# Row halves of TensorE taken in turn in a time mix, and value rows split three tiles ahead in an expert layer

## Chip, cores and metric

One core of one Trainium2 chip runs the whole program. The metric is the device time of one execution in microseconds; lower is better. Three timed executions of the kernel before took 3079.56, 3082.31 and 3094.72 us.

## The reference

Two transformer blocks over 512 tokens of width 1024, in float32. The first has attention, a convolution branch and a product-key expert layer (16,384 experts, 8 heads, top 16). The second has a linear-recurrence time mix (RWKV-7), a sparse attention (NSA), a gated merge and a convolutional feed-forward. Two parts matter here:

```python
# expert layer, for a chunk of 128 tokens
u = peer_u[e]                                  # e: 16 experts for each of 8 heads
h = gelu(einsum('cd,chkd->chk', xc, u))
return einsum('chk,chkd->cd', g * h, peer_v[e])

# time mix, for every token
sa = einsum('bhvk,bhk->bhv', state, a_t)
state = state * w_t + sa[..., None] * b_t + v_t[..., None] * k_t
y_t = einsum('bhvk,bhk->bhv', state, r_t)
```

The expert layer is computed densely for three of the four token tiles (all 16,384 experts, with a gate matrix that is zero nearly everywhere) and by gathers for the fourth. The time mix is computed in chunks of 128 tokens: products of the keys, queries and decays under a triangular mask, the inverse of a triangular matrix for each chunk and head, and a state that goes from chunk to chunk.

## The kernel before, in words

The program is written with a tile framework. Each engine has its own queue in order; the order of the queues is planned at compile time by a simulated time line over the program order, and tiles with a number of buffers (`bufs`) make their next user wait until an old one is free. PSUM is cut into eight banks: four with the tag `pb`, two `mm`, two `po`.

Matmuls at full precision split their operands in a high and a low part (float32r) and take three products, `mm3` (L264 to L266). A plain float32 matmul appears in the trace as two records, each with its own weight load.

**Expert layer** (`peer`). The 16,384 experts are 128 tiles of 128. In the loop at the end of `peer`, a group of four tiles at a time, `up` makes the weighted gelu of the next group (by matmuls L264 to L266, or from a tile that was computed ahead and stored, `gh_d`), splits it (L817, L818) and calls `slot_up`, a gather and a dot product for the fourth token tile (L779, L788). Then `v_split(et + 1)` splits the next tile of value rows: ScalarE casts two halves (L676), GpSimd and VectorE subtract (L677), and the next load is issued on SyncE's queue (L666). The split tiles have two buffers each (`vh`, `vl`, L673); the raw rows have three. Then 18 matmuls (L844) accumulate the tile into six banks, and `slot_down` gathers a value row for each token and adds it (L796). `weights(gi + 1)` loads the gates of the next group (L800), with two buffers. Before the loop, the first split is done when the routing of the last token tile is known (L743).

**Time mix** (`Rwkv`). Heads of 64 come in pairs, so a tile of 128 rows holds two heads, the even one (`par` 0) in rows 0 to 63 and the odd one in rows 64 to 127.
- `pair` makes the inputs of two heads for all four chunks. At its end (L1464 to L1471) each `par` takes a bank, four matmuls over 64 rows, and a masked multiply into `LT`.
- `invert` inverts the triangular blocks: by VectorE up to 32 x 32, then by matmuls over 32 rows (L1529, L1534, L1536) and over 64 rows (L1545, L1549). The 32-row part goes over two quads (rows 0 to 63, and 64 to 127) and, in each, over two chunks with a bank each.
- `front` prepares a chunk without the state; its helper `lower` (L1580) does three masked products, each for both `par` in turn: a bank, four matmuls over 64 rows (L1586), a masked multiply on VectorE (L1588), and a `yield`. `times_v` (L1597) uses the results. `back` does what needs the state. `chunks` runs `back` of one chunk in turns with `front` of the next.

Beside it, projections for the sparse attention (L264 to L266, `side` and `plain` in `block2`) are given out in portions behind each chunk, and the keys of the attention are prepared (`Nsa.keys`: L1765 to L1822) once `invert` has freed its memory.

Of the kernel before, what the change touches and what calls it, by code (L numbers as in the profile page):

```python
# [9 lines left out]
F32R = mybir.dt.float32r  # L10
# [8 lines left out]
P = 128  # L19
S = 512  # L20
D = 1024
# [515 lines left out]
SD = ND * P  # L537
NE = 128
GE = 4
VRAW = 3  # L540
NA = 68
TB = 32
NSLOT = 128
# [14 lines left out]
def peer(c, st, st_u, last):  # L558
# [20 lines left out]
    for half, cs in enumerate(HALVES):  # L579
# [3 lines left out]
        for k in range(KD):  # L583
            if half and k % 4 == 0:
                tp = c.bank()
            hn, h, lo = c.t2("hn")[:, 0:256], xh[k][:, cs], xl[k][:, cs]
# [42 lines left out]
    for hd in range(8):  # L629
        for half in range(2):  # L630
            if 2 * hd + half < NQH:
                ps = first[2 * hd + half][0]
            else:
                ps = c.bank("mm", 2)
# [25 lines left out]
    ng = NE // GE  # L660
# [7 lines left out]
    def v_split(et):  # L668

        if et >= NE:  # L670
            return
        r = vraw.pop(et)
        h, lo = (vp.tile([P, D], F32R, name=f"v{n}{et}", tag=f"v{n}", bufs=2) for n in "hl")  # L673
        for e in range(2):
            s = slice(e * 512, (e + 1) * 512)
            nc.scalar.copy(h[:, s], r[:, s])  # L676
            (nc.vector if e % 2 else nc.gpsimd).tensor_sub(lo[:, s], r[:, s], h[:, s])  # L677
        vsplit[et] = (h, lo)
        v_load(et + VRAW)


    for i in order:
# [55 lines left out]
        if i == order[-1]:  # L738
            esE.close()
            vp = esB.open("c8", 2)  # L740
            for et in range(VRAW):
                v_load(et)
            v_split(0)  # L743

        gf, gs = c.sm("gf", [P, P], bufs=1), c.sm("gs", [P, 2, P], F16, bufs=2)
        nc.scalar.activation(gf, tr[:, 2 * P:3 * P], AF.Copy, scale=GSCALE)
# [49 lines left out]
        nc.vector.scalar_tensor_tensor(acc, v, ghs[gi][:, s:s + 1], acc, op0=OP.mult, op1=OP.add)  # L796

    def weights(gi):
        wt = c.sm("wt", [P, GE * SD], bufs=2).rearrange("p (b e t) -> p b e t", b=SD // TB, e=GE)
        nc.sync.dma_start(wt, w_d[:, :, gi * GE:(gi + 1) * GE, :].rearrange("b p e t -> p b e t"))  # L800
        return wt

# [17 lines left out]
        slot_up(gi, e)  # L820

    ahead(NA - NB)
    wt = weights(0)
    for e in range(GE):
        up(0, e, wt)
    ahead(NB)
    acc = esB.open("gat", 1, side="right").tile([P, D], F32, name="acc", tag="acc")
    nc.gpsimd.memset(acc, 0.0)

    outs = [[c.bank(("po", "pb", "pb")[i]) for _ in range(2)] for i in range(ND)]  # L830
    for gi in range(ng):
        if gi + 1 < ng:
            wt = weights(gi + 1)
        for e in range(GE):
            et = gi * GE + e
            if gi + 1 < ng:
                up(gi + 1, e, wt)
            v_split(et + 1)
            vs, ps = vsplit.pop(et), acts.pop(et)
            for i in range(ND):  # L840
                ts = slice(i * P, (i + 1) * P)
                for n, (a, v) in enumerate(((0, 0), (0, 1), (1, 0))):
                    for half in range(2):
                        nc.tensor.matmul(outs[i][half], ps[a][:, ts], vs[v][:, half * 512:(half + 1) * 512],  # L844
                                         start=et == 0 and n == 0, stop=et == NE - 1 and n == 2)
            slot_down(gi, e)
# [511 lines left out]
class Rwkv:  # L1358
# [52 lines left out]
    def pair(self, cj, r, k, v):  # L1411
# [49 lines left out]
        nc.gpsimd.tensor_mul(k, k, e2)  # L1461
        nc.gpsimd.tensor_mul(a, a, e2)
        nc.vector.scalar_tensor_tensor(kk, kk, -1.0, e3, op0=OP.mult, op1=OP.mult)
        for par in range(2):  # L1464
            rows = slice(par * 64, par * 64 + 64)
            ps = self.bank()
            for n in range(4):
                cs = slice(n * P, (n + 1) * P)
                nc.tensor.matmul(ps[:, cs], a[rows, cs], kk[rows, cs], start=True, stop=True)
            nc.vector.tensor_mul(self.LT[g][:, :, par * 4 + j], ps.rearrange("p (n t) -> p n t", n=4),  # L1470
                                 up_s[:, None, :].to_broadcast([P, 4, P]))  # L1471
        for w, t in enumerate((kk, r, k, a, v, rkr)):
# [3 lines left out]
    def invert(self, g):  # L1476
# [38 lines left out]
        for n0 in (0, 2):  # L1515
            st = []
            for n in (n0, n0 + 1):
                u0, pt = n * 8, PT[n]
                q64 = self.sm("q64", [P, 8, 64], bufs=2)
                nc.gpsimd.memset(q64, 0.0)  # L1520
                for b in range(4):
                    s = slice(b * 32, b * 32 + 32)
                    nc.gpsimd.tensor_copy(q64[s, :, (b % 2) * 32:(b % 2) * 32 + 32], Qc[s, u0:u0 + 8, :])
                    nc.vector.tensor_copy(pt[s, :, s], Pc[s, u0:u0 + 8, :])
                st.append((u0, pt, q64, c.bank("po", 2), self.sm("zz", [P, 8, 32], bufs=2)))
            for q0, q1 in quads:
                for u0, pt, q64, z1, zz in st:
                    for u in range(8):
                        nc.tensor.matmul(z1[q1, u * 32:(u + 1) * 32], pt[q0, u, q1], Qc[q0, u0 + u, :], start=True, stop=True)  # L1529
                    nc.vector.tensor_copy(zz[q1], z1[q1, 0:256].rearrange("p (u i) -> p u i", u=8))  # L1530
            for q0, q1 in quads:
                for u0, pt, q64, z1, zz in st:
                    for u in range(8):
                        nc.tensor.matmul(z1[q1, 256 + u * 32:256 + (u + 1) * 32], Pc[q1, u0 + u, :], zz[q1, u, :],  # L1534
                                         start=True, stop=True)
                        nc.tensor.matmul(z1[q0, 256 + u * 32:256 + (u + 1) * 32], zz[q1, u, :], Pc[q1, u0 + u, :],  # L1536
                                         start=True, stop=True)
                    nc.vector.tensor_copy(q64[q1, :, 0:32], z1[q1, 256:512].rearrange("p (u i) -> p u i", u=8))
                    nc.vector.tensor_copy(pt[q0, :, q1], z1[q0, 256:512].rearrange("p (u i) -> p u i", u=8))
            z3s = []  # L1540
            for u0, pt, q64, z1, zz in st:
                z3, z6 = c.bank("po", 2), self.sm("z6", [P, 8, 64], bufs=2)
                z3s.append((z3, z6))
                for u in range(8):
                    nc.tensor.matmul(z3[hi, u * 64:(u + 1) * 64], pt[lo, u, hi], q64[lo, u, :], start=True, stop=True)  # L1545
                nc.vector.tensor_copy(z6[hi], z3[hi, :].rearrange("p (u i) -> p u i", u=8))
            for (u0, pt, q64, z1, zz), (z3, z6) in zip(st, z3s):
                for u in range(8):
                    nc.tensor.matmul(z3[lo, u * 64:(u + 1) * 64], z6[hi, u, :], pt[hi, u, hi], start=True, stop=True)  # L1549
                nc.vector.tensor_copy(pt[lo, :, hi], z3[lo, :].rearrange("p (u i) -> p u i", u=8))  # L1550
                nc.sync.dma_start(self.pt_d[u0 // 8][g], pt.rearrange("p u t -> p (u t)"))
        self.pp = pp

    def front(self, g, n):
# [24 lines left out]

        def lower(lhs, rhs, msk, tag):  # L1580
            r = []
            for par in range(2):
                rows = slice(par * 64, par * 64 + 64)
                ps = self.bank()
                for j in range(4):
                    nc.tensor.matmul(ps[:, j * P:(j + 1) * P], lhs[rows, j], rhs[rows, j], start=True, stop=True)  # L1586
                t = self.sm(tag, [P, 4, P], 4 if tag == "rb" else 2)
                nc.vector.tensor_mul(t, ps.rearrange("p (j t) -> p j t", j=4), msk[:, None, :].to_broadcast([P, 4, P]))  # L1588
                r.append(t)
                yield  # L1590
            return r
# [484 lines left out]
```

## Time and profile before

| what | value |
|---|---|
| median of three timed executions | 3082.31 us |
| the profiled execution | 3063.27 us |
| its span, first to last instruction | 3061.3 us |
| TensorE, VectorE, GpSimd, ScalarE busy | 2855.0, 2309.1, 1806.8, 1208.4 us |
| mean granted TensorE clock | 0.957 |

Busy time of an engine is the union of its instructions; the ends of matmuls are modelled, so they lie over each other, and the time from one matmul's start to the next one's is what a matmul takes of TensorE. PE is TensorE's matmul, PEld its weight load, DVE VectorE, ACT ScalarE, POOL GpSimd, SP SyncE; a q behind it is the queue itself. "A <- B" among the waits is A's engine standing idle until B.

The stages are, from the span's start: the first block's attention and convolution and the routing up to about 840 us, the expert loop to about 1660, the time mix's inputs to about 1980, its inversion and chunks to about 2320, the sparse attention to about 2540, then the merge and the feed-forward.

### The profile page before, as it was taken

Reading aid. Unit: us, or ns where it says so; the run is one execution under the profiler, and the core shown is the slowest. Engines: PE = TensorE matmul, PEld = TensorE weight load, DVE = VectorE, ACT = ScalarE, POOL = GpSimd, SP = SyncE. Lnnn points to the kernel's source line nnn. Section 1 sums busy time; section 2 is a strip of 40 time slices with the busy share of each in tenths; the row PEclk is TensorE's granted clock in tenths of the full one; section 3 lists DMA queues with packets and bytes.
Section 4 is the critical chain, followed back from the end, with each engine's and each line's share of the span. In section 5 each row is a group of like instructions: output and inputs, shape, how many; then the busy total and the mean of one; then the engine's idle time right before and its main releaser. Section 6 shows DMA issues by size and latency. Waiting matters only on the chain. (4 is left out here: it accounts for less than half of the span.)

```text
span 3061.3 us, 42565 instructions
## 1 busy us (share of the span) xinstructions
PE 2855.0 (93%) x15507; PEld 2433.8 (80%) x15507; DVE 2309.1 (75%) x3734; ACT 1208.4 (39%) x2077; POOL 1806.8 (59%) x1231
## 2 busy tenths in 40 slices
PE   6789997889999999999999899899999998999998
PEld 5557897779978888888887677688887877888887
DVE  7985899997188999999998688968345874477721
ACT  4444334456333333333334432211225764444431
POOL 5544465543667888888885376623347754554444
PEclk9789998999999999999999999998999999999999
DMA  3101244446799999999996555453753226322232
GB/s 131 41 14 57 77 129 127 173 156 249 237 338 316 327 335 335 323 324 341 332 336 212 177 161 165 139 172 104 222 159 99 76 70 214 120 90 93 93 96 76
DMA packets 270918, 554.01 MB, mean 181 GB/s; under 512 B 41394, under 2 KB 147890, under 8 KB 268916
## 3 DMA queue, kind: packets, MB, share of 16 engines
q1 hardware_dynamic: 219264, 370.91, 37.8%
q0 software_dynamic: 36864, 134.23, 12.0%
q10 hardware_dynamic: 14580, 46.15, 4.2%
q8 instruction: 122, 2.00, 0.3%
q14 instruction: 88, 0.72, 0.1%
HBM read 464.77 MB, written 83.89 MB: 179 GB/s over the span
## 5 line engine op out<-in xcount | busy, mean ns | idle before, releaser
L247 POOL TENSOR_TENSOR wl<-wr,wh 128x1024 fp32r<-128x1024 f32 x319 | 812.9, 2550 | 557.8 <-ACT wh L245 297.9
L245 ACT CAST wh<-wr 128x1024 fp32r<-128x1024 f32 x319 | 334.7, 1050 | 611.5 <-PE mm L265 201.3
L788 DVE CUSTOM_DVE_ANT_0 ur<-ur,hnt 128x1024 f32<-128x1024 f32 x128 | 216.8, 1695 | 74.2 <-DMA ur<-in_u,eix 72.9
L779 POOL DMA_INDIRECT ur<-in_u,eix x128 | 169.5, 1324 | 63.7 <-DVE hc L788 34.4
L677 POOL TENSOR_TENSOR vl<-vr,vh 128x512 fp32r<-128x512 f32 x128 | 190.9, 1492 | 23.6 <-ACT vh L676 18.1
L677 DVE TENSOR_TENSOR vl<-vr,vh 128x512 fp32r<-128x512 f32 x128 | 183.4, 1433 | 25.8 <-issue 16.8
L796 DVE SCALAR_TENSOR_TENSOR acc<-vr,hc,acc 128x1024 f32<-128x1024 f32 x128 | 193.5, 1512 | 1.8 <-DMA vr<-in_vrow,eix 1.7
L779 POOL DMA_INDIRECT vr<-in_vrow,eix x128 | 155.5, 1215 | 47.1 <-issue 24.0
L676 ACT CAST vh<-vr 128x512 fp32r<-128x512 f32 x256 | 145.6, 619 | 76.2 <-issue 31.1
L844 PE MATMUL pb<-vl,ah 128*128 128x512 f32 x512 | 168.9, 397 | 0.0
L844 PE MATMUL pb<-vh,al 128*128 128x512 f32 x512 | 166.4, 395 | 0.0
L844 PE MATMUL pb<-vh,ah 128*128 128x512 f32 x512 | 163.1, 399 | 2.4 <-ACT ah L817 2.4
L766 PE MATMUL pb<-og,o 128*128 128x128 f16 x768 | 105.8, 296 | 41.6 <-DVE og L761 41.2
L766 PEld LDWEIGHTS <-o 128*128 128x128 f16 x768 | 82.7, 119 | 59.6 <-DVE og L761 28.5
L768 ACT ACTIVATE wb<-pb 128x512 f32<-128x512 f32 x96 | 98.9, 1139 | 71.6 <-PE pb L766 71.1
L353 DVE SCALAR_TENSOR_TENSOR acc<-hp,vecs,acc 128x512 f32<-128x512 f32 x100 | 115.8, 1173 | 0.7
L844 PEld LDWEIGHTS pb<-vh,ah 128*128 128x128 f32 x512 | 97.3, 190 | 23.7 <-ACT ah L817 2.7
L844 PEld LDWEIGHTS pb<-vl,ah 128*128 128x128 f32 x512 | 97.2, 190 | 23.0
L844 PEld LDWEIGHTS pb<-vh,al 128*128 128x128 f32 x512 | 97.2, 190 | 22.9
L758 DVE TENSOR_TENSOR o<-iota,sl 128x1024 f16<-128x1024 f16 x96 | 105.4, 1126 | 11.1 <-ACT sl L737 6.9
L1927 POOL TENSOR_TENSOR prob<-prob,nz 128x128 f32<-128x128 f32 (+3 forms) x128 | 88.6, 724 | 39.4 <-DVE nz L1924 27.6
L1152 DVE TENSOR_TENSOR tot<-tot,sq 128x512 f32<-128x512 f32 x11 | 17.0, 1548 | 112.9 <-ACT sq L1149 112.9
(1404 smaller groups left out, 8991.0 us busy)
## 6 DMA issues: line engine op xcount, KB each, us to landing
wr<-in_ws SPq DMA_DIRECT2D x191, 512.0 KB
wr<-in_uT SPq DMA_DIRECT2D x128, 512.0 KB
vr<-in_vrow SPq DMA_DIRECT2D x128, 512.0 KB
w_d<-wb ACTq DMA_DIRECT2D x12, 2048.0 KB
wt<-w_d SPq DMA_DIRECT2D x32, 768.0 KB
gh_d<-gh ACTq DMA_DIRECT2D x68, 192.0 KB
gh<-gh_d SPq DMA_DIRECT2D x68, 192.0 KB
rd_d<-z SPq DMA_DIRECT2D x24, 256.0 KB
```

Of the source, the lines that this page charges most:

```text
L245: c.nc.scalar.copy(h, r)
L247: eng.tensor_sub(lo, r, h)
L353: nc.vector.scalar_tensor_tensor(acc[j], hp[:, tap:tap + S], w[:, tap:tap + 1], acc[j], op0=OP.mult, op1=OP.add)
L676: nc.scalar.copy(h[:, s], r[:, s])
L677: (nc.vector if e % 2 else nc.gpsimd).tensor_sub(lo[:, s], r[:, s], h[:, s])
L758: nc.vector.tensor_tensor(o, iota4[:, None, :, :].to_broadcast(shape), by4(sl[:, a, ts]), op=OP.is_equal)
L766: nc.tensor.matmul(wp[:, u * P:(u + 1) * P], o2[:, q, :, u], og[n][:, q, :, u], start=n == 0, stop=n == 1)
L768: nc.scalar.activation(wb[:, :, t4:t4 + 4].rearrange("p e t -> p t e"), wp.rearrange("p (t e) -> p t e", t=4), AF.Copy, scale=1.0 / GSCALE)
L779: nc.gpsimd.indirect_dma_start(out=t, out_offset=None, in_=src, in_offset=bass.IndirectOffsetOnAxis(ap=eix[:, s:s + 1], axis=0))
L788: nc.vector.tensor_tensor_reduce(out=u, in0=u, in1=hnt, scale=1.0, scalar=0.0, op0=OP.mult, op1=OP.add, accum_out=hc[:, s:s + 1])
L796: nc.vector.scalar_tensor_tensor(acc, v, ghs[gi][:, s:s + 1], acc, op0=OP.mult, op1=OP.add)
L844: nc.tensor.matmul(outs[i][half], ps[a][:, ts], vs[v][:, half * 512:(half + 1) * 512], start=et == 0 and n == 0, stop=et == NE - 1 and n == 2)
```

## The change

Four places in the time mix put the two row halves in turn: in `pair` and in `lower` both halves take their bank first, the matmuls alternate between the halves, and the two masked multiplies come behind all of them; in `invert` the 32-row matmuls go over two "turns", each with a different quad for each of the two chunks, alternating from matmul to matmul, with the copies behind. In the expert layer the value rows are split three tiles ahead instead of one, with four buffers instead of two, three splits before the loop instead of one, and the gates are loaded two groups ahead instead of one.

```diff
+VAHEAD = 3
...
-        h, lo = (vp.tile([P, D], F32R, name=f"v{n}{et}", tag=f"v{n}", bufs=2) for n in "hl")
+        h, lo = (vp.tile([P, D], F32R, name=f"v{n}{et}", tag=f"v{n}", bufs=VAHEAD + 1) for n in "hl")
...
-            v_split(0)
+            for et in range(VAHEAD):
+                v_split(et)
...
-        wt = c.sm("wt", [P, GE * SD], bufs=2).rearrange("p (b e t) -> p b e t", b=SD // TB, e=GE)
+        wt = c.sm("wt", [P, GE * SD], bufs=3).rearrange("p (b e t) -> p b e t", b=SD // TB, e=GE)
...
-    wt = weights(0)
+    wts = [weights(0), weights(1)]
...
-        if gi + 1 < ng:
-            wt = weights(gi + 1)
+        if gi + 2 < ng:
+            wts.append(weights(gi + 2))
...
-            v_split(et + 1)
+            v_split(et + VAHEAD)
...
-        for par in range(2):
-            rows = slice(par * 64, par * 64 + 64)
-            ps = self.bank()
-            for n in range(4):
-                cs = slice(n * P, (n + 1) * P)
+        pss = [self.bank() for _ in range(2)]
+        for n in range(4):
+            cs = slice(n * P, (n + 1) * P)
+            for par, ps in enumerate(pss):
+                rows = slice(par * 64, par * 64 + 64)
                 nc.tensor.matmul(ps[:, cs], a[rows, cs], kk[rows, cs], start=True, stop=True)
+        for par, ps in enumerate(pss):
             nc.vector.tensor_mul(self.LT[g][:, :, par * 4 + j], ps.rearrange("p (n t) -> p n t", n=4),
...
-            for q0, q1 in quads:
-                for u0, pt, q64, z1, zz in st:
-                    for u in range(8):
+            turns = [[(quads[(a + b) % 2], st[a]) for a in range(2)] for b in range(2)]
+            for turn in turns:
+                for u in range(8):
+                    for (q0, q1), (u0, pt, q64, z1, zz) in turn:
                         nc.tensor.matmul(z1[q1, u * 32:(u + 1) * 32], pt[q0, u, q1], Qc[q0, u0 + u, :], start=True, stop=True)
+                for (q0, q1), (u0, pt, q64, z1, zz) in turn:
                     nc.vector.tensor_copy(zz[q1], z1[q1, 0:256].rearrange("p (u i) -> p u i", u=8))
-            for q0, q1 in quads:
-                for u0, pt, q64, z1, zz in st:
-                    for u in range(8):
+            for turn in turns:
+                for u in range(8):
+                    for (q0, q1), (u0, pt, q64, z1, zz) in turn:
                         nc.tensor.matmul(z1[q1, 256 + u * 32:256 + (u + 1) * 32], Pc[q1, u0 + u, :], zz[q1, u, :],
                                          start=True, stop=True)
+                    for (q0, q1), (u0, pt, q64, z1, zz) in turn:
                         nc.tensor.matmul(z1[q0, 256 + u * 32:256 + (u + 1) * 32], zz[q1, u, :], Pc[q1, u0 + u, :],
                                          start=True, stop=True)
+                for (q0, q1), (u0, pt, q64, z1, zz) in turn:
                     nc.vector.tensor_copy(q64[q1, :, 0:32], z1[q1, 256:512].rearrange("p (u i) -> p u i", u=8))
...
-            for par in range(2):
-                rows = slice(par * 64, par * 64 + 64)
-                ps = self.bank()
-                for j in range(4):
+            pss = [self.bank() for _ in range(2)]
+            for j in range(4):
+                for par, ps in enumerate(pss):
+                    rows = slice(par * 64, par * 64 + 64)
                     nc.tensor.matmul(ps[:, j * P:(j + 1) * P], lhs[rows, j], rhs[rows, j], start=True, stop=True)
+            for ps in pss:
                 t = self.sm(tag, [P, 4, P], 4 if tag == "rb" else 2)
                 nc.vector.tensor_mul(t, ps.rearrange("p (j t) -> p j t", j=4), msk[:, None, :].to_broadcast([P, 4, P]))
```

## Rows read from the trace of the kernel before

**Rows 1.** Stage and length, us; busy PE, PEld, DVE, ACT, POOL; clock, DMA share, GB/s.
```profile
840.00:1660.00 820.00, 802.61 (x3783) 693.75 (x3784) 757.34 (x789) 288.74 (x534) 664.84 (x438) 0.99 0.91 323
...
1780.00:1880.00 100.00, 100.00 (x508) 83.35 (x507) 88.84 (x92) 28.98 (x47) 77.20 (x53) 1.00 0.57 164
1880.00:1980.00 100.00, 84.27 (x406) 68.17 (x405) 92.17 (x116) 21.94 (x38) 57.24 (x37) 0.90 0.53 151
1980.00:2080.00 100.00, 96.90 (x918) 81.80 (x917) 71.31 (x123) 17.04 (x27) 33.44 (x28) 0.92 0.46 152
...
2180.00:2320.00 140.00, 137.68 (x855) 119.01 (x855) 50.11 (x114) 41.23 (x74) 65.40 (x46) 0.96 0.59 172
```
**Rows 2.** TensorE's groups, 1780 to 2300: xcount | busy us, mean ns | idle before.
```profile
L1586 PE MATMUL pb<-ar,ck 64*128 64x128 f32 x384 | 49.3, 293 | 0.0
...
L1469 PE MATMUL pb<-kk,a 64*128 64x128 f32 x128 | 14.3, 293 | 3.2 <-DVE kk L1463 3.2
...
L1536 PE MATMUL po<-c4y,zz 32*32 32x32 f32 x256 | 10.5, 193 | 0.0
...
L1529 PE MATMUL po<-c4y,LT 32*32 32x32 f32 x256 | 10.1, 194 | 0.0
```
**Rows 3.** TensorE's time line in pieces: start, duration, line, shape, records merged.
```profile
2023.32 0.48 PE L1586 MATMUL pb<-ar,ck 64*128 64x128 f32 x2
2023.73 0.59 PE L1529 MATMUL po<-c4y,LT 32*32 32x32 f32 x13
...
2028.92 0.19 PE L1534 MATMUL po<-zz,c4y 32*32 32x32 f32 x2
...
2028.95 0.19 PE L1534 MATMUL po<-zz,c4y 32*32 32x32 f32 x2
...
2031.42 1.16 PE L1586 MATMUL pb<-ar,ck 64*128 64x128 f32 x8
2032.51 0.21 PE L1534 MATMUL po<-zz,c4y 32*32 32x32 f32 x1
...
2124.10 1.19 PE L1529 MATMUL po<-c4y,LT 32*32 32x32 f32 x32
2125.22 1.16 PE L1586 MATMUL pb<-ar,ck 64*128 64x128 f32 x10
2126.32 1.55 PE L1645 MATMUL pb<-X,PT 128*128 128x64 f32 x12
...
2132.76 1.71 PE L1586 MATMUL pb<-ar,ck 64*128 64x128 f32 x16
2134.40 0.94 PE L1652 MATMUL pb<-U,tokb 128*128 128x128 f32 x6
```
**Rows 4.** VectorE's masks after the chunk products, 1980 to 2320, columns as before.
```profile
L1588 DVE TENSOR_TENSOR A<-pb,rk 128x512 f32<-128x512 f32 x32 | 21.1, 684 | 12.2 <-PE pb L1586 12.0
```
**Rows 5.** A wait in the chunks, 1980 to 2320: us in total, times, longest.
```profile
PE pb L1597 <- DVE A L1588: 6.9, 3, 4.7
```
**Rows 6.** Waits in the expert loop, 836 to 1664, columns as before.
```profile
ACT vh L676 <- PE pb L844: 22.3, 22, 3.0
...
PE po L844 <- POOL vl L677: 6.3, 5, 2.3
...
PE po L844 <- ACT vh L676: 5.3, 2, 2.9
...
PE po L844 <- DVE vl L677: 3.5, 3, 2.0
```
**Rows 7.** Busy time just ahead of the expert loop, and the page's group of VectorE's splits.
```profile
770.00:840.00 70.00, 69.57 (x402) 69.25 (x400) 8.68 (x9) 22.36 (x32) 43.73 (x21) 1.00 0.72 230
...
L677 DVE TENSOR_TENSOR vl<-vr,vh 128x512 fp32r<-128x512 f32 x128 | 183.4, 1433 | 25.8 <-issue 16.8 <-ACT vh L676 8.6
```
**Rows 8.** The chain that ended last, in 2165 to 2340: start, us, what.
```profile
2178.12 9.23 DMA cw<-in_cw
...
2279.10 2.72 DMA kz<-nk_d
```

More of the change, by code (lines that the diff above doesn't have):

```diff
@@ L822, in peer @@
     ahead(NA - NB)
-    wt = weights(0)
+    wts = [weights(0), weights(1)]
     for e in range(GE):
-        up(0, e, wt)
+        up(0, e, wts[0])
     ahead(NB)
@@ L836, in peer @@
             if gi + 1 < ng:
-                up(gi + 1, e, wt)
-            v_split(et + 1)
+                up(gi + 1, e, wts[gi + 1])
+            v_split(et + VAHEAD)
             vs, ps = vsplit.pop(et), acts.pop(et)
```

## The prediction

> **What bounds the kernel now.** I read the page's busy times first: TensorE is busy 2855.0 us of 3061.3, 93%, so less work for TensorE can shorten the run wherever no other engine sets the pace. Busy time by stage says where that is [rows 1]. In the expert loop (840 to 1660) TensorE is busy 802.61 of 820 us, VectorE 757.34, and DMA's share is 0.91: three resources near their limit, with TensorE idle for 17.4 us. In the time mix TensorE is busy 100 of 100 us, then 84.27 (here VectorE leads, with 92.17), then 96.90 of 100 and, past one more stretch of that kind, 137.68 of 140, where VectorE has 71.31 and 50.11. So from 1980 to 2320 TensorE's work is the bound; the masks wait for it, 12.0 us, rather than it for them [rows 4]. The waits say what TensorE lacks in the expert loop: halves of the split value rows [rows 6].
>
> **The change part by part.**
>
> *Chunk products (L1586).* 384 records, 49.3 us of TensorE [rows 2]: 24 sets (8 chunks x 3 products), each of two row halves x 4 matmuls x 2 records. The time line gives the price of a run of records, from its start to the next instruction's [rows 3]: 8 records 1.09 us (2031.42 to 2032.51), 10 records 1.10 (2125.22 to 2126.32), 16 records 1.64 (2132.76 to 2134.40). Ten cost what eight cost: where a run passes from one half to the other, records of both are under way at once, and 16 cost 1.64 and not 2.18 because that happens only around the passage. With the halves alternating, each half's 8 records lie beside the other's, and a set costs about what 8 do: 24 x 1.10 = 26.4 us. TensorE gains 49.3 - 26.4 = 22.9 us. Bounds: if alternating brings no more than the runs of 16 already have, 24 x 1.64 = 39.4, a gain of 9.9; if each of the 192 matmuls pays what a lone one does (2 records, 2023.32 to 2023.73, 0.41 us), 78.7, a loss of 29.4. I take 22.9, by the nearest rows (8 against 10 records).
>
> The Trainium skill (TensorE: Matmul & The Clock Gate, Part 3, Measured speedup vs the span model) states 3.07 times for four row tiles, less than four. Held to the same share, two would give 1.54 of 2, and by my estimate the gain would be 49.3 - 24 x 2.18 / 1.54, about 15 us. The 8 and 10 record rows show no such loss.
>
> Not all of it reaches the end. Both halves' masks (VectorE, 0.684 us each [rows 4]) now come behind both products, 1.37 us in a row, where the first half's could lie beside the second's matmuls. A chain of product, masks, next product is 1.10 + 1.37 = 2.47 us against 1.64 + 0.68 = 2.32: no shorter. The gain exists because TensorE fills that wait with projections (L264 to L266), which wait for none of this. Where the compiled order has none at the place, TensorE waits for the mask, as it does now for 6.9 us [rows 5]. I let that wait about double, 6 us more, and count 17. If the cover is gone everywhere, one more mask a set stands in the open, 24 x 0.684 = 16.4 us, and 6.5 are left. Each product also takes two of four PSUM banks at once; they come back by the same masks, so this wait is in the same bound.
>
> *Pair products (L1469).* 8 sets of 16, 14.3 us [rows 2]; at 1.10 each 8.8, a gain of 5.5. Half of them lie where TensorE is full (1780 to 1880), the others mostly where VectorE leads [rows 1]: I count 3. Bounds by the same rows: from a loss of 64 x 0.41 - 14.3 = 11.9 to the gain of 5.5.
>
> *Inversion (L1529, L1534, L1536).* 32 records of L1529 take 1.12 us (2124.10 to 2125.22); all 256 take 10.1 [rows 2, 3]. L1534 and L1536 alternate between output columns already and lie beside each other in about 10.5. At 2028.92 and 2028.95, where two such runs of different rows meet, the time line has two records of L1534 to a place instead of one [rows 3]. Doubled all along, the two groups fall by 5 each, a gain of 10. Nothing shows that this pace holds for long, so the other bound is 0; a loss is excluded, since both runs are under way at once there. I take 4. The copies behind them are as many as before, in pairs.
>
> *Value rows three ahead.* TensorE waits at L844 for vl, 6.3 and 3.5 us, and for vh, 5.3 [rows 6]: 15.1 us for the split of the next value tile. That tile has two buffers and can only start when the tile two back is used; ScalarE waits for that 22.3 us in 22 times [rows 6]. With four buffers and three tiles of 820 / 128 = 6.4 us ahead, a late split has 19 us to spare, and the 15.1 us go. What is late next: VectorE, 757.34 of then 805 us, 94%, and DMA, whose 0.91 rises to 0.93. Behind a waiting cast on ScalarE stand the casts of weights and gelu tiles, as before: the slot that it waits for is again that of the tile before the current one. The raw rows' next load waits on SyncE's queue for the split, and behind it stand the loads of weights, gates and gelu tiles: the same distance too. I count 11 us; bounds 0 (VectorE takes over) and the 17.4 of idle time. The two further splits before the loop fall into 770 to 840, where VectorE is busy 8.68 of 70 us [rows 7]: nothing; without that cover two subtractions of 1.433 us, 2.9. The gates a group earlier are one 768 KB load moved ahead in SyncE's queue; TensorE waits for none of them: 0, at worst one DMA of the length seen elsewhere, 9.23 us [rows 8], behind which a weight load stands once.
>
> Sum: 17 + 3 + 4 + 11 = 35 us. The profiled execution took 3063.27 us, 1.97 more than its span and 19 less than the median of 3082.31. On its scale the forecast is 3028, on the median's 3047.
>
> **The rivals.**
>
> *The time mix hangs on another chain.* From 2178 to 2282 the chain that ended last runs through the loads for the compressed keys (cw, 9.23 us, to the last kz) and only in part through TensorE [rows 8]. They start when the inversion frees its memory, so they move only by what the inversion saves. For it: that chain, and the longer masks. The Trainium skill (TensorEngine Tiling, PSUM Bottleneck) warns that tiling speeds up TensorE and not the evacuation of PSUM, and the masks' 1.37 us against 1.10 of product agree. Against it: TensorE stays full to 2320 [rows 1], 38 us past the last of these loads, so the stage can lose its 24 us before they bind. Time: the loop's 11 and the inversion's 4 are left, 3067, within what a measurement can tell from no change (0.5%, 15 us).
>
> *Only the time mix gains.* VectorE and DMA hold the loop as it is: 3082 - 24 = 3058.
>
> *A change of rows restarts the array.* This one ends on the other side: if each alternation has to finish the matmul before, L1586 and L1469 pay the lone price, 29.4 + 11.9 us more. It decides as soon as a set costs 11 / 32 = 0.34 us more than its 1.64, since then the loop's gain is eaten. With the loop's 11: 3082 + 30 = 3112. For it: 0.41 us for a lone matmul. Against it: 10 records in 1.10. With it I put a worse order of the queues, which the compiler plans anew around larger pools and for which no row speaks.
>
> **How the numbers follow.** Forecast (a gain of 31 to 56) 0.5; only the time mix (16 to 31) 0.2; another chain 0.2; restart or a worse order 0.1. So faster 0.70, same 0.20, slower 0.10. The range's low end is TensorE's whole sum, 22.9 + 5.5 + 10 + 17.4 = 55.8, with the spread of the runs: 3022. Its high end takes in the other chain and the mild half of what is worse: 3085.
>
> **What would show it.** Right: sets of 16 records of L1586 in about 1.1 us; L1529's 32 records in less than 0.8; TensorE's waits for vl and vh under 3 us; the loop about 11 us shorter, and 1980 to 2320 about 20. Wrong: sets at 1.6 us or more; over 10 us of new waits of TensorE for masks or banks; a loop as long as before, with VectorE the fuller; or a later stage that gives back what these two gain.

## The result

Ratios carry a 95% interval.

| | before | after | ratio |
|---|---|---|---|
| median of five executions each | 3082.31 us | 3050.30 us | 0.9911 [0.9882, 0.9940] |
| again, 11 and 6 executions | 3078.98 us | 3044.38 us | 0.9884 [0.9859, 0.9909] |
| the profiled execution, its span | 3063.27, 3061.3 us | 3043.09, 3041.3 us | |

Forecast were 3047 us, 35 us less. The medians fell by 32.0 and 34.6 us, the two profiled executions differ by 20.2. Where the 20 lie is read from five moments of the two traces, in us from the span's start:

| moment | before | after | stage before | stage after |
|---|---|---|---|---|
| first matmul of the expert loop | 841.9 | 849.2 | 841.9 | 849.2 |
| end of the loop (next matmul after its last) | 1662.3 | 1656.2 | 820.3 | 807.0 |
| first chunk product | 2012.4 | 2002.3 | 350.1 | 346.0 |
| first scores of the sparse attention | 2322.3 | 2301.1 | 309.9 | 298.8 |
| end | 3061.3 | 3041.3 | 739.1 | 740.3 |

The loop gives 13 us where 11 were forecast, the inputs 4 where 3 were, and the chunks 11 where 21 were (17 and 4); the stretch ahead of the loop takes 7, for which the forecast had 0; what follows is as before. Some of the expectations below end the loop earlier, at the first copy of its sums out of PSUM (1661.1 before, 1653.4 after). That mark moves by itself: it comes 1.2 us ahead of the loop's end before and 2.8 after, because the last matmuls stand in another order, and by it the loop would seem to gain 15. Busy time by stretch in the profile after (columns as in [rows 1]):

```profile
690.00:770.00 80.00, 74.55 (x498) 68.81 (x497) 66.44 (x73) 52.33 (x64) 30.71 (x13) 0.94 0.67 243
770.00:847.00 77.00, 77.00 (x450) 76.99 (x448) 7.62 (x9) 27.68 (x38) 45.83 (x22) 1.00 0.77 249
847.00:1654.00 807.00, 798.04 (x3787) 693.87 (x3786) 767.70 (x787) 279.04 (x532) 669.79 (x436) 1.00 0.93 327
1783.00:1880.00 97.00, 94.83 (x484) 78.52 (x484) 87.76 (x89) 31.88 (x55) 72.24 (x51) 1.00 0.60 170
...
1970.00:2070.00 100.00, 93.67 (x944) 79.00 (x942) 77.34 (x134) 17.99 (x28) 39.37 (x30) 0.95 0.51 164
...
2160.00:2299.00 139.00, 135.96 (x847) 116.48 (x846) 49.59 (x111) 40.87 (x73) 64.58 (x45) 0.96 0.56 170
```

In the loop TensorE's idle time fell from 17.4 us to 9.0; VectorE's share rose to 95% and DMA's to 0.93, where the prediction had 94% and 0.93.

TensorE's time line after, in pieces (start, duration, line, shape, records merged), answers [rows 3]:

```profile
1781.34 1.16 PE L1472 MATMUL pb<-kk,a 64*128 64x128 f32 x16
1782.43 1.05 PE L1428 MATMUL pb<-sqm,tmp 128*128 128x2 f32 x8
...
2006.25 1.16 PE L1596 MATMUL pb<-ar,ck 64*128 64x128 f32 x8
2007.34 0.43 PE L1608 MATMUL pb<-tokv,A 128*128 128x64 f32 x2
...
2009.67 0.48 PE L1596 MATMUL pb<-ar,ck 64*128 64x128 f32 x2
2010.09 1.77 PE L1608 MATMUL pb<-tokv,A 128*128 128x64 f32 x14
...
2101.04 0.78 PE L1535 MATMUL po<-c4y,LT 32*32 32x32 f32 x32
2101.75 0.66 PE L1583 MATMUL pb<-sqm,ck 128*128 128x128 f32 x4
...
2249.76 1.16 PE L1596 MATMUL pb<-ar,ck 64*128 64x128 f32 x16
2250.85 2.00 PE L1656 MATMUL pb<-X,PT 128*128 128x64 f32 x16
```

From start to next start, sixteen records of the pair and chunk products (L1472, L1596) take 1.09 us where they took 1.64, and 32 of L1535 take 0.71 where they took 1.12. But the chunk products also have runs of eight at 1.09: one half alone, then the other. In the compiled order, counted by the banks that the matmuls write, 13 of the 24 sets alternate all along, 7 are in the old order (four matmuls of one half, four of the other), and 4 are mixed. Start to next start, all records of the pair products take 8.8 us (13.7 before), of the chunk products 39.8 (48.3; the forecast for them was 26.4), of L1535 6.2 (9.2), of L1541 with L1544 8.0 (10.8). That is 19 us less for TensorE.

TensorE's waits after, in the loop (847 to 1654) and then in the chunks (1970 to 2301), in us, times, longest, answer [rows 6] and [rows 5]:

```profile
PE mm L266 <- POOL wl L247: 2.6, 2, 2.5
...
PE po L846 <- POOL vl L678: 1.2, 2, 0.6
PE po L846 <- DVE vl L678: 1.2, 1, 1.2
```
```profile
PE pb L1583 <- DMA ck<-rd_d: 4.6, 2, 4.4
PE pb L1608 <- DVE A L1599: 3.5, 3, 2.0
PE pb L1705 <- ACT tokv L1585: 2.1, 1, 2.1
```

The 15.1 us of waits for vh and vl are 2.4, and ScalarE's wait for the slot (22.3 us) is gone; waits for a weight half (wl, 2.6 us) and for gelu halves (ah, 3.5, where 2.4 were) stand in the loop now. In the chunks the wait for a mask is 3.5 us (6.9 before); new are a load of chunk operands that comes too late (ck, 4.6 us) and a wait for tokv.

### The profile page after: what moved, and what is told of

Same layout as the page of the kernel before. It is cut to its first block, busy times and chain, and to the rows that moved or that the text cites. A ratio compares the mean times of both kernels' runs of the same rounds, so it can differ in the third digit from the quotient of the medians.

```text
span 3041.3 us, 42532 instructions
## 1 busy us (share of the span) xinstructions
PE 2838.8 (93%) x15507; PEld 2421.6 (80%) x15507; DVE 2328.0 (77%) x3734; ACT 1201.2 (39%) x2077; POOL 1817.2 (60%) x1231
## 5 line engine op out<-in xcount | busy, mean ns | idle before, releaser
L790 DVE CUSTOM_DVE_ANT_0 ur<-ur,hnt 128x1024 f32<-128x1024 f32 x128 | 231.8, 1811 | 69.9 <-DMA ur<-in_u,eix 66.3
L678 POOL TENSOR_TENSOR vl<-vr,vh 128x512 fp32r<-128x512 f32 x128 | 191.7, 1498 | 13.6 <-ACT vh L677 12.2
L781 POOL DMA_INDIRECT vr<-in_vrow,eix x128 | 163.3, 1276 | 45.4 <-issue 23.6
L678 DVE TENSOR_TENSOR vl<-vr,vh 128x512 fp32r<-128x512 f32 x128 | 169.0, 1322 | 15.3 <-issue 14.4
L846 PE MATMUL pb<-vl,ah 128*128 128x512 f32 x512 | 160.6, 394 | 0.0
L846 PE MATMUL pb<-vh,al 128*128 128x512 f32 x512 | 160.2, 394 | 0.0
L819 ACT CAST ah<-mm 128x384 fp32r<-128x384 f32 x60 | 28.8, 480 | 217.3 <-DVE mm L817 210.1
L1938 POOL TENSOR_TENSOR prob<-prob,nz 128x128 f32<-128x128 f32 (+3 forms) x128 | 88.7, 725 | 39.1 <-DVE nz L1935 23.5
```

The source lines that it names most:

```text
L781: nc.gpsimd.indirect_dma_start(out=t, out_offset=None, in_=src, in_offset=bass.IndirectOffsetOnAxis(ap=eix[:, s:s + 1], axis=0))
L790: nc.vector.tensor_tensor_reduce(out=u, in0=u, in1=hnt, scale=1.0, scalar=0.0, op0=OP.mult, op1=OP.add, accum_out=hc[:, s:s + 1])
```

## The experiments

Two things are compared throughout: stages of one profile each, and the timed executions. Those of before spread over 37 us (3061.88 to 3099.08), and go with TensorE's mean granted clock in each. So a straight line was laid through span and mean clock of 121 executions (12 kernels, 53 executions of before; a constant for each kernel, one common slope; all +- are 95% intervals): the span falls by 22.7 +- 2.3 us for each 0.01 of mean clock, with 3.7 us left as scatter. The constants, at a clock of 0.955 and as a difference to before, are taken for what the work itself is worth; they are named "at equal clock" below. What sets the clock stays out of such a fit.

**Time mix alone** (L1464 to L1471, L1526 to L1549 and L1582 to L1591 changed, the expert layer as before).

Against the kernel after:

```diff
-            for et in range(VAHEAD):
-                v_split(et)
+            v_split(0)
...
-            v_split(et + VAHEAD)
+            v_split(et + 1)
```


> The time mix part alone, the expert layer as before. My theory, that the two parts add up without touching each other: nothing changes up to 1660 us, and from there to the end of the chunks the kernel is 14 to 15 us shorter, as between the traces of before and after; span about 3047 against 3061. Rival, that the gain of the time mix hangs on the earlier start of the stage or on the order planned with the larger pools: under 5 us or over 25 us. In both the pair products (L1469 before) take 1.09 us for 16 records.

3056.15 us against 3081.59: 0.9917 [0.9890, 0.9943]; at equal clock -13.9 +- 3.0 us. In its profile the loop is 819.5 us, as before, and sixteen records of the pair products take 1.09. Its span, 3060.2, isn't the 3047 expected: the chunk stage is 311.4 us, longer than in the profile of before, with 61.4 of them at the lower clock (37.5 in before). What the time mix is worth is read from the timed executions, then, and by them the rival that leaves it the inversion's 4 us alone is out.

**Expert layer alone.**

Against the kernel after, here for the chunk products; the pair products and the inversion likewise:

```diff
-            pss = [self.bank() for _ in range(2)]
-            for j in range(4):
-                for par, ps in enumerate(pss):
-                    rows = slice(par * 64, par * 64 + 64)
+            for par in range(2):
+                rows = slice(par * 64, par * 64 + 64)
+                ps = self.bank()
+                for j in range(4):
```


> The expert part alone, the time mix as before. My theory: 6 us are lost between 690 and the start of the loop, where splits of two more value tiles lie among the last gate block, and 13 us are gained in the loop, so span about 3055 against 3061, which three rounds can hardly tell from no change; the loop starts near 849 instead of 842 and its first stage after it 6 us earlier. Rival: the loss ahead of the loop was chance of one profile, then the loop starts at 842 to 844 and the span is about 3048.

3079.81 us: 0.9975 [0.9945, 1.0005]; at equal clock -10.4 +- 2.5. The two parts add up: 13.9 + 10.4 = 24.3, and the whole change has -24.6 +- 2.5. The median shows little of the 10, since this kernel's mean clock was the lowest (0.9491 in 10 executions; 0.9513 in 53 of before). Its profile has the loop's start at 848.7 us, as expected, and the loop at 810.7; its span is 3080.1 and not about 3055, for the chunk stage takes 332.9. Three stretches of that stage (columns as in [rows 1]):

```profile
2113.00:2123.00 10.00, 10.00 (x108) 8.46 (x108) 8.57 (x25) 1.64 (x2) 5.50 (x7) 1.00 0.23 92
2123.00:2147.00 24.00, 24.00 (x236) 22.56 (x236) 8.98 (x21) 2.44 (x5) 5.01 (x11) 0.50 0.14 45
2147.00:2171.00 24.00, 24.00 (x161) 21.33 (x161) 6.83 (x12) 1.77 (x3) 2.54 (x2) 0.50 0.40 132
```

For 48 us the granted clock is 0.50, 1.2 GHz of 2.4, with TensorE busy all the time, and busy all the 10 us before. The chunk code of this kernel is that of before, whose own profile has 37.5 us at the lower level in that stage, the longest piece 10.2. The next two kernels below also have four value buffers beside the old chunk code, and the same piece of 47.8 us: it begins 114 us after the first chunk product in all three, where the two profiles of before have pieces of 10.2 and 30.7 us from 82 us on. So these stretches go with the kernel and not with the run alone.

**Four buffers alone.**

```diff
-        h, lo = (vp.tile([P, D], F32R, name=f"v{n}{et}", tag=f"v{n}", bufs=2) for n in "hl")
+        h, lo = (vp.tile([P, D], F32R, name=f"v{n}{et}", tag=f"v{n}", bufs=4) for n in "hl")
```


> The kernel before with four buffers for the split value tiles and nothing else: the split is still asked for one tile ahead, with one before the loop, and the gates come one group ahead. If the buffers are what frees the loop (the compiled order moves a split up as soon as a buffer is free), the loop falls from 819 us to 804 to 808 and starts near 848 as in the changed kernel. If the distance of three tiles in the program is needed, the loop stays at 816 to 820.

The loop is 811.2 us (807.1 by the mark of the expectation), as in the expert part as a whole (810.7), though the program still asks for the split one tile ahead: the compiler's planner moves the split up as soon as a buffer is free. The start of the loop is late here too (849.5). So by this profile the gain and the early loss both belong to the buffers; one execution took 3078.62 us.

**Gates one group ahead, as before.**

```diff
-        wt = c.sm("wt", [P, GE * SD], bufs=3).rearrange("p (b e t) -> p b e t", b=SD // TB, e=GE)
+        wt = c.sm("wt", [P, GE * SD], bufs=2).rearrange("p (b e t) -> p b e t", b=SD // TB, e=GE)
...
-        if gi + 2 < ng:
-            wts.append(weights(gi + 2))
+        if gi + 1 < ng:
+            wts.append(weights(gi + 1))
```


> The expert part alone as in e2_expert, but with the gates one group ahead and two buffers for them as before. My theory, that the gates' earlier load does nothing for TensorE: the loop takes 805 to 810 us as in e2_expert (807.9). Rival, that the two waits for the group's first gelu halves and gates are part of the gain: 812 to 816.

In the expert part alone: the loop is 807.3 us, against 810.7 with the gates early (804.4 and 807.8 by the mark of the expectation). Their earlier load brings nothing that one profile shows.

**Third and fourth split held back.** The whole change, with these two splits put behind the last cast of the gates in the queues.

```diff
-            for et in range(VAHEAD):
+            for et in range(2):
                 v_split(et)
...
+    with tc.issue_after(gate.ins):       # gate: the last cast of the gates
+        for et in range(2, VAHEAD):
+            v_split(et)
...
-            v_split(et + VAHEAD)
+            with tc.issue_after(gate.ins) if et == 0 else ExitStack():
+                v_split(et + VAHEAD)
```


> The changed kernel, but the splits of the third and fourth value tile are held back behind the last cast of the gate block (the first two stay where they were before the change). If these splits among the gate block are what cost 5 to 6 us ahead of the loop, the loop starts near 843 to 844 instead of 849, its gain stays 13, and the span is 3035 to 3037 against 3041. Rival: the loss comes from the loads of value rows or of the gates ahead of time; then the loop still starts near 848 to 849 and the span stays at 3041.

The loop starts at 841.3 us, where it did before the change. The prediction had put the added splits into 770 to 840. Without this hold they come earlier, among the one-hot gate matrices of 690 to 770, as ScalarE's casts show. Two tiles are split there before the change and four after it, two casts each; these are the casts behind the first tile's (first the kernel before, then after):

```profile
711.25 1.18 ACT L676 CAST vh<-vr 128x512 fp32r<-128x512 f32 x2
```
```profile
713.04 1.18 ACT L677 CAST vh<-vr 128x512 fp32r<-128x512 f32 x2
714.94 0.61 ACT L677 CAST vh<-vr 128x512 fp32r<-128x512 f32 x1
715.45 0.62 ACT L677 CAST vh<-vr 128x512 fp32r<-128x512 f32 x1
723.74 1.14 ACT L677 CAST vh<-vr 128x512 fp32r<-128x512 f32 x2
```

There TensorE waits for VectorE. That wait in 690 to 770, in the kernel before, after, and with the hold:

```profile
PE pb L766 <- DVE og L761: 1.1, 2, 0.8
```
```profile
PE pb L768 <- DVE og L763: 5.4, 4, 2.9
```
```profile
PE pb L768 <- DVE og L763: 1.1, 2, 0.8
```

Over all profiles the loop starts at 845.8 to 849.5 us in the six that have the early splits (mean 847.8), and at 840.5 to 848.8 in the eight that have not (mean 843.3): the early splits cost about 5 us. The two groups overlap only in the 848.8 (the chunk products alone), which has more time at the lower clock ahead of 690 than any other (143.4 us, the others 119.5 to 136.5). From 690 to the loop they are apart: TensorE is idle for 6.3 to 7.3 us in the six and 2.2 to 3.7 in the eight, and 10.2 to 13.7 us lie at the lower clock against 3.4 to 6.8. Timed: 3043.08 us, 0.9872 [0.9819, 0.9926], at equal clock -27.3 +- 3.8; the profile's span is 3055.2 and not 3035 to 3037, with 64.9 us of the chunk stage at the lower clock (27.3 in the first profile after).

**Alternation forced.** The whole change, with each matmul of a chunk product bound behind the one before it in TensorE's queue.

```diff
+            prev = None
...
-                    nc.tensor.matmul(ps[:, j * P:(j + 1) * P], lhs[rows, j], rhs[rows, j], start=True, stop=True)
+                    with c.tc.issue_after(prev.ins) if prev else ExitStack():
+                        prev = nc.tensor.matmul(ps[:, j * P:(j + 1) * P], lhs[rows, j], rhs[rows, j], start=True, stop=True)
```


> The changed kernel, but in the chunk products each matmul of one half is ordered behind the one before it of the other half, so that the compiled order can't put a half's four matmuls in a row. In the changed kernel 384 records took 39.8 us from start to next start, with some sets one half after the other, where 24 sets at 1.1 would be 26.4. My theory, that the compiled order lost the alternation: they take 29 to 33 us and the chunks end 5 to 9 us earlier, span 3033 to 3037. Rival, that a half waits for its bank and TensorE stands idle for it: the records get cheaper but waits of TensorE grow by as much, span 3039 to 3045.

All 24 sets alternate, and yet the 384 records take 37.7 us, 2.1 less than in the change and more than expected. Three lines of its time line, from three places, tell why:

```profile
2001.30 0.49 PE L1598 MATMUL pb<-ar,ck 64*128 64x128 f32 x2
...
2019.54 0.71 PE L1598 MATMUL pb<-ar,ck 64*128 64x128 f32 x8
...
2050.82 2.08 PE L1598 MATMUL pb<-ar,ck 64*128 64x128 f32 x16
```

The 24 sets lie in 37 runs, cut by other matmuls that the planner puts between. Nine runs are a lone pair of records, at 0.41 us for what costs 0.14 within a set (1.09 / 8). Four matmuls that alternate cost 0.64 (2019.54 to the next start), not half of 1.09. Some sets fall into stretches at 1.2 GHz (the last line), and one run's 4.82 us hold a wait for a mask (3.66). With two shorter ones, 4.7 us of the 37.7 are waits, and none of the 39.8 in the change are: the records themselves got 6.8 us cheaper, and most of it went into waiting, which is what the rival forecast. Its span came too (3039.8), but not its reason, since the longest wait is for a mask and not for a bank. So the order inside a set was one of several reasons. 3041.87 us, 0.9880 [0.9827, 0.9932]; at equal clock -28.4 +- 3.9.

**Both repairs together**, the edits of the last two.

> The changed kernel with both repairs: the third and fourth value split held behind the gate block, and the chunk products ordered to alternate. Each alone was timed at 0.987 to 0.988 of before, the changed kernel at 0.991. My theory, that both repairs act in different stages and add: 0.984 to 0.986, 3033 to 3038 us; the loop starts near 842, its length stays near 807, the chunk products stay under 38 us. Rival, that what is won ahead of the loop is lost again in the chunks, whose length varies with the granted clock from run to run: 0.987 to 0.990.

3051.85 us, 0.9910 [0.9880, 0.9941]; at equal clock -25.0 +- 2.8, against -24.6 +- 2.5 for the change itself. The ratio lies above what theory and rival forecast. The profile has the loop's start (842.3 us) that was expected and a loop of 806.6; the chunk products take 39.6 us, not under 38, and the chunk stage 311.9, of which 61.4 are at the lower clock. The repairs don't add up, and none of the three kernels is shown to beat the change; the version to keep is the change as it is.

**Chunk products alone, and inversion alone**, each in the kernel before.

```diff
-            for par in range(2):
-                rows = slice(par * 64, par * 64 + 64)
-                ps = self.bank()
-                for j in range(4):
+            pss = [self.bank() for _ in range(2)]
+            for j in range(4):
+                for par, ps in enumerate(pss):
+                    rows = slice(par * 64, par * 64 + 64)
```


> The kernel before with only the chunk products alternating (pair products, inversion and expert layer as before). In this compiled order 11 of 24 sets alternate, 9 not at all, 4 in part. My theory, that this is the larger part of the time mix's gain (all of it together was timed at 0.9917): 0.994 to 0.996, some 12 to 18 us. Rival, that the inversion carries it, since the inversion's end releases the memory for the next stage's loads: 0.997 to 1.000 here.

```diff
-            for q0, q1 in quads:
-                for u0, pt, q64, z1, zz in st:
-                    for u in range(8):
+            turns = [[(quads[(a + b) % 2], st[a]) for a in range(2)] for b in range(2)]
+            for turn in turns:
+                for u in range(8):
+                    for (q0, q1), (u0, pt, q64, z1, zz) in turn:
...
```


> The kernel before with only the inversion's 32-row matmuls in turns. My theory: the three kinds of matmuls fall from 20 us to 14 as in the changed kernel, 4 to 6 us of the run, 0.998 to 0.9985, which three rounds can't tell from no change. Rival, that the inversion carries the time mix's gain, because its end releases the next stage's loads: 0.994 to 0.996.

Chunk products: 3072.39 us, 0.9975 [0.9950, 1.0001]; at equal clock -3.6 +- 2.5. Their records take 44.5 us here (48.3 in before, 39.8 in the change), and 11 of the 24 sets alternate. Inversion: 3064.73 us, 0.9956 [0.9926, 0.9986]; at equal clock -5.8 +- 2.7. Both medians fell into the range of the rival, by which the inversion carries the gain; at equal clock the two intervals overlap, and which is worth more isn't shown. The rival's reason isn't seen either: the first load that the inversion's end releases (cw) is issued 167.3 us after the first chunk product here, and 162.4 and 171.9 us after it in the two profiles of before. In the one profile of the inversion the chunk stage isn't shorter (315.9 us, 44.4 of them at the lower clock), so where its gain lies is not shown.

**Rows or banks?** The pair products of the kernel before, rows in sequence, with the bank alternating from matmul to matmul.

```diff
-            ps = self.bank()
+            pss = [self.bank() for _ in range(2)]
...
-                nc.tensor.matmul(ps[:, cs], a[rows, cs], kk[rows, cs], start=True, stop=True)
+                nc.tensor.matmul(pss[n % 2][:, (n // 2) * P:(n // 2 + 1) * P], a[rows, cs], kk[rows, cs], start=True, stop=True)
```


> The kernel before, where only the pair products differ: the four matmuls of a half still come in a row, but their outputs alternate between two PSUM banks (each half has two banks, half full; the masked multiplies are four of half the size). If the rows are what lets matmuls run at once, a set of 16 records keeps its 1.64 us (128 records about 13.5 in all). If another bank is what does it, it falls to about 1.1 us as in the changed kernel (8.8 in all).

```profile
1791.07 1.71 PE L1469 MATMUL pb<-kk,a 64*128 64x128 f32 x16
1792.70 0.50 PE L264 MATMUL mm<-xg7h,wh 128*128 128x512 f32 x1
```

Sixteen records take 1.64 us (the median of eight sets), as before: another bank alone brings nothing, the other rows are needed. Whether two halves would lie beside each other in one bank wasn't tried. One execution took 3081.95 us. Its inputs' stage is 17 us longer than in before (366.9 us), and its chunks begin that much later with less left to do, so its stages stay out of the comparisons below; what makes it longer was not followed up.

**Before and after once more.**

> The kernel before once more, for the granted clock in the chunks. The same chunk code took 309.9 us with 37 us at the lower clock in the profile of before, and 332.9 with 89 in e2_expert. My theory, that a stretch of the chunks costs half of its time at the lower clock and that this time varies from run to run: chunks between 305 and 335 us, and 290 plus or minus 3 us once half of the time at the lower clock is taken off. Rival, that the longer chunks of e2_expert came with its start 4 us earlier: 308 to 312 with 35 to 40 us at the lower clock.

> The changed kernel once more, in five rounds, for its ratio and its chunks. By the profiles of one run each the change is worth 20 us, by the medians 27 to 32. My theory, that the profile of before had little time at the lower clock in the chunks: the ratio is 0.988 to 0.992 again, and the chunks take 282 to 286 us once half of their time at the lower clock is taken off, 5 to 8 less than before. Rival, that the change also shortens the time at the lower clock: 20 to 40 us of it again, where before has 60 to 90.

The profile of before taken again has the chunk stage at 320.5 us, 58.0 of them at the lower clock (309.9 and 37.5 in the first); that of after 306.2, with 47.8 (298.8 and 27.3). TensorE fills this stage, and sixteen records take 2.00 us at the lower level (2050.82 above, to the next start) and 1.09 at the upper, so the length less half of the time at the lower level can be compared: 288.6 to 291.5 us in the five profiles with the old chunk code and inversion, 280.7 to 285.1 in the six with the new ones. Means: 290.6 and 282.8, 7.8 us less. The kernel with the chunk products alone has 285.6 by this count, and the one with the inversion alone 293.8. For before, the length and the 290 came as expected, and the rival's 308 to 312 did not.

## Why the prediction came out

The time was right: 3047 forecast, 3050.3 and 3044.4 measured. The sum was not right in all its terms, and that the time agrees is partly luck. At equal clock the work became 24.6 +- 2.5 us shorter, not 35. About 8 more go with the clock, which the sum didn't hold: its mean was 0.9513 +- 0.0010 before (53 executions) and 0.9547 +- 0.0014 after (11), and 0.0034 at 22.7 us for each 0.01 is 7.7. Of the prediction's signs the pace of a set, the waits for value halves and the loop came; the 20 us between 1980 and 2320 did not (11 in the profiles, 7.8 less by the means above). Term by term:

- **Value rows, 11 us (0 to 17.4): right.** The loop is 818.8 to 821.2 us in the six profiles with two buffers and 806.6 to 811.2 in the eight with four; means 820.3 and 808.7, 11.6 less. The waits that were to go went; TensorE's idle time, by the same ends, is 15.3 us in the mean of the six and 8.9 in that of the eight, so it holds 6.4 of the 11.6. That VectorE would take over, the rival that held the loop as it is, is refuted at 95% busy. The distance in the program, on which the working rested (19 us to spare), is not what did it: the buffers alone did.
- **The early splits, 0 us (2.9 without cover): wrong.** They cost about 5. The step that failed is "fall into 770 to 840": the planner put them where the raw rows and the buffers were ready, 46 to 55 us earlier, among the gates' one-hots, for which TensorE waits. The 2.9 was mis-sized as well, since it counted the subtractions and not what they hold up (below).
- **The chunk products, 17 us (22.9 on TensorE): mis-sized, the largest error.** The pace was right to the digit, 1.09 us a set. But it assumed that the queue would hold the order of the program: 13 of 24 sets do, and others are cut. TensorE gained 8.5 us on them where 22.9 were forecast (9.4 by the second profiles, 51.3 and 41.9). Alone, in an order where TensorE gained 3.8, they are worth 3.6 +- 2.5; of the time mix's 13.9 the inversion and the pair products leave them 4 to 5. The mask waits, for which 6 us were taken off, did not double: 3.5 us in the first profile after, 6.8 in the second, 6.9 before. The group of masks that answers [rows 4] waits 16.0 us for products, more than the 12.2 before:

```profile
L1599 DVE TENSOR_TENSOR A<-pb,rk 128x512 f32<-128x512 f32 x32 | 21.2, 685 | 16.0 <-PE pb L1596 15.9
```

  The other group of masks (rb) waits 9.8 us, where it waited 15.2. So the masks still wait for the products, and the time mix rival's evidence, masks longer than products, did not come to bear; new waits came elsewhere, 4.6 us (2.2 in the second profile) for a load of ck that comes after TensorE is ready for it.
- **Pair products, 3 us: right.** The stage of the inputs is 348.5 to 350.3 us in the seven profiles with the old pair products as they were, 343.0 to 347.9 in the six with the new ones; means 349.4 and 345.8, 3.6 less.
- **Inversion, 4 us (0 to 10): right in size.** TensorE takes 5.8 us less for its 32-row matmuls, and alone it is worth 5.8 +- 2.7. Its one profile doesn't show it (293.8 us by the count above, against 288.6 to 291.5), so the size rests on the timed executions.
- **The rival of the array that restarts** is refuted: a set that alternates costs 1.09, below its 1.64. The lone pair's 0.41, on which it rested, is real where a set is cut.
- **Another chain** (the loads of [rows 8]) does not bind: in 2150 to 2320 the chain after runs through TensorE, with three pieces of DMA:

```profile
2185.05 2.89 DMA gt_d<-o
...
2242.35 6.71 DMA ck<-rd_d
...
2300.62 3.98 DMA bg<-rd_d
```

- **Not in the sum: the clock.** The kernels with new time mix code alone had a mean of 0.9566 (whole, 8 executions), 0.9555 (inversion) and 0.9536 (chunk products), against 0.9513 of before; the expert part alone 0.9491. Why TensorE's clock goes with these edits is not settled. The stages' means, 11.6, 3.6 and 7.8 less the 4.5 ahead of the loop, give 18.5 of the 24.6 +- 2.5; where the rest lies no profile here shows. The prediction also put its profile 19 us under the median and went by that difference; but that profile's clock was 0.957, above the mean of 0.9513, so part of what the medians lost was never in its rows.

The Trainium skill (TensorE: Matmul & The Clock Gate, Part 3, Measured speedup vs the span model) has 3.07 for four row tiles, and the prediction weighed 1.54 for two. The trace shows no such loss for two halves: eight records of one half take 1.09 us, and sixteen of both take 1.09.

## What to carry to other kernels

An order of instructions in the program is a wish: where a planner fills the queues, count in the compiled order how many sets keep it before pricing the gain. More buffers move work ahead by themselves, also to places where another engine waits for the one that does it; look for the first free buffer, not for the line. A stage's end is its last instruction, not the first use of its result, which moves with the order. Where executions spread with the granted clock, compare them at equal clock: here the parts then add up to the whole, which the medians hide.

## What was not expected of the hardware

A VectorE operation on half-precision one-hots that takes 0.69 us by itself takes 2.8 when GpSimd has begun a subtraction of float32 tiles just before. VectorE and GpSimd in the kernel before:

```profile
703.22 2.81 DVE L758 TENSOR_TENSOR o<-iota,sl 128x1024 f16<-128x1024 f16 x1
...
707.39 0.69 DVE L758 TENSOR_TENSOR o<-iota,sl 128x1024 f16<-128x1024 f16 x1
```
```profile
703.09 2.39 POOL L247 TENSOR_TENSOR wl<-wr,wh 128x1024 fp32r<-128x1024 f32 x1 [1.25 <-ACT wh L245]
```

VectorE's operation ends at 706.03, 0.55 us after GpSimd's (705.48): it looks as if it stood still meanwhile. Of the 64 such operations between 690 and 770 in this profile, eight took 1.53 to 2.90 us; each began while GpSimd was subtracting, and each ended 0.55 us after that subtraction. Two more began under the longest subtraction (4.15 us) and took 0.68; the other 54 began under none and took at most 0.70. So what such a meeting costs can be read off: about the rest of GpSimd's operation. The Trainium skill (SBUF — State Buffer, SBUF: two separate sides) says that the two engines share a pair of ports under an exclusive lock, which a VectorE operation with two SBUF inputs needs too; the trace agrees, with 2.1 us lost. GpSimd's subtraction there is one of weights, and most of the others are too, before the change and after it. After the change two more value subtractions stand among these operations: under one of them two operations take 2.24 us together instead of 1.29, and TensorE then waits 2.87 for the result:

```profile
727.38 2.24 DVE L763 TENSOR_TENSOR og<-o,gs 128x1024 f16<-128x1024 f16 x2
```
```profile
726.77 1.71 POOL L678 TENSOR_TENSOR vl<-vr,vh 128x512 fp32r<-128x512 f32 x1
```
```profile
729.07 0.40 PE L768 MATMUL pb<-og,o 128*128 128x128 f16 x2 [2.87 <-DVE og L763]
```

The other wait that is new in that stretch (1.50 us at 750.87) lies behind a subtraction of weights.

And the same chunk code ran with 37.5 to 88.7 us at 1.2 GHz in one stage of some 320 us, in three kernels with one piece of 48 us and TensorE never idle in it, shown above for one of them.
